# A gated-DeltaNet layer with its out-projection moved behind all heads and two column pairs in seven block products

## The chip, the core and the metric

The kernel runs on one core of one Trainium2 chip. Its time is device microseconds from one launch; the median of three runs counts. Five engines work beside each other and are tied by semaphores: TensorE (PE, matrix products into PSUM), VectorE (DVE), ScalarE (ACT), GpSimd (POOL) and SyncE (SP), whose queue issues every DMA of this kernel in order.

## The reference, cut to what matters

A trunk of two residual layers on x of 1024 tokens by 1024 features, float32, and a final RMSNorm. Layer 0 is a gated DeltaNet (GDN), layer 1 an mLSTM. Each has 8 heads with keys and queries of width 128 and values of width 256.

```python
def gdn_mixer(h, w_in, conv_w, a_log, dt_bias, norm_w, w_out):
    p = h @ w_in                                   # q, k: 1024 columns each; v, z: 2048 each; a, b: 8 each
    ...
    qkv = silu(causal_dwconv(qkv, conv_w))         # 4 taps
    q = l2norm(q) * HEAD_QK ** -0.5;  k = l2norm(k)
    g = -exp(a_log) * softplus(a + dt_bias);  beta = sigmoid(bt)
    o = gated_delta_chunked(q, k, v, g, beta)      # S_t = exp(g)(I - beta k k^T) S_{t-1} + beta k v^T; o = S^T q
    o = rmsnorm(o, norm_w) * silu(z)               # per head
    return o.reshape(B, T, D_INNER) @ w_out        # 2048 x 1024
...
for i in range(DEPTH):
    x = x + mixer_i(rmsnorm(x, norm_w[i]), ...)
return rmsnorm(x, final_norm_w)
```

## The kernel before, in words

Activations lie features first, in tiles of 128 features by 512 tokens: `x[k][half]`, k from 0 to 7, two halves. Every float32 operand of a large product is split into a high part (`hi`, fp32r) and a low part (`lo`, the rest), and a product is three matmuls, hi x hi, hi x lo and lo x hi. `split` (lines 255 to 261) makes the parts of a weight: the high part on ScalarE, the low part on GpSimd. `prenorm` (244) writes the parts `h_hi` and `h_lo` of the normed input.

**One GDN head** projects q, k, two column tiles of v and two of z (`proj_half`, 272: 8 contraction tiles x 3 matmuls for one column tile and half). `conv_silu` (288) reads the sum out of PSUM and does the four taps on VectorE. `gdn_prepare` (536) transposes q and k, forms k k^T and k q^T for eight chunks of 128 tokens and sends the diagonal 32x32 blocks through DRAM (`nt_dram`, then `nd`). `gdn_solve` (606) inverts them with 62 dependent VectorE instructions (lines 615 and 617), sends the result through DRAM (`tb`), and `gdn_merge` (621) joins the blocks to whole 128x128 inverses in four levels of small matmuls (`xp`, `yp`, `xl`, `yl`, line 645). `gdn_scan` (676) then goes over the eight chunks in a chain: `ks` (k times the state S, 702) -> `rr` (VectorE, 704) -> `y` (708) -> `w` (ScalarE, 710) -> `sn` (724) -> the new state `S` (VectorE, 729), with the output `o` (733, 734) beside it. `gate_chunk` (359) transposes a finished chunk, multiplies by the norm weight and silu(z), and splits it into `gg_hi` and `gg_lo`. `out_part` (382) multiplies a half of the head's gated values by the head's 256 rows of the out weights and adds each of eight PSUM tiles into x (VectorE, 399). So the out-projection is done head by head, each a half behind its scan.

**What sets the order.** TensorE's instructions run in the order in which the program emits them (`manual_schedule`); a scheduler orders the other engines. In the GDN layer the order comes from a planner: `gdn_head` is a generator over the next head's units, and between two steps of a scan `pump` takes as many of them as a budget in nanoseconds allows (constants `FA`, `FB`, `FC`; 4500 behind a state), while `out(n)` takes steps of the out-projection. A unit that must wait for a tile names a gate ("mid", "v0", "end", "merge"), which the scan opens. When the next head's units run out, the merge runs with what is left of z between its levels (`ZG`).

**The mLSTM layer** has another form. Its projections are `Pair`s (957): two column tiles, two halves of the tokens and two halves of the contraction make a 2x2 product of blocks, done in seven block products of 12 matmuls (`product`, 949) instead of eight. The sums of input blocks `S1` to `S4` are built once (`h_blocks`, 920, and `last_block`, 938), in the tiles of x, which is kept in DRAM meanwhile; the sums of weight blocks are built per pair. Its out-projection for heads 0 to 6 comes behind all heads (`out_heads`, 1357), from gated values that were stored in DRAM, accumulated over the heads in PSUM. Lists of step numbers (`FIRST`, `UNITS`) say after which block product which piece of scan or preparation comes.

Of the kernel before, what the change touches and what calls it, by code (L numbers as in the profile page):

```python
# [34 lines left out]
PLACES = ((35, 39, 41, 44, 45, 47, 49, 51), (20, 31, 34, 36, 37, 40, 43, 46))  # L35
DECAY = 34
VLO = (((1, 3, 6, 7), (1, 2, 3, 5, 7)), ((3, 6, 7), (1, 3, 5, 7)))
ZM = (24, 17, 15)
ZG = (2, 1, 1)
SECOND = (4, 9)  # L40
P1 = ((), ())
NORM1 = ((-1, 1, 4), (-1, 9, 15))
AHEAD = 6500
MF = 900
RATE0 = 0.5
FS = 1280
OE = 6
ON = (2, 2, 0, 0, 0)
OL = (2, 1, 0, 0, 1)
FA = 600  # L50
FB = 900
FC = 4500
LA = 300
LB = 300
LC = 1280
QB, KB = 4, 3
WB, GB = 2, 2
EP = 0
VT = "ccpp", "ccbb"
B0, B1 = "dc", "d"  # L60
ORDER = "o0 a0 h1 b0 o4 a4 o6 a6 b4 b6"
R8 = range(8)
LOOK = 2
FIRST = {0: "g", 13: "g", 18: "g", 23: "g", 28: "g", 33: "p", 37: "p", 42: "b", 46: "b", 50: "b", 54: "bp", 60: "pr", 68: "s",
# [3 lines left out]
          **{u: "ss" for u in (13, 15, 17, 19, 21, 24, 26)}, 28: "s"})  # L68
# [6 lines left out]
def hybrid_kernel(ctx, tc, x_in, norm_w, final_norm_w, gdn_w_in, gdn_conv_w, gdn_a_log, gdn_dt_bias, gdn_norm_w,  # L75
# [40 lines left out]
    def load_q(w, name):  # L116

        raw = hp.tile([P, KT, P], F32, tag="gate", bufs=GB, name=f"{name}_raw")
        nc.sync.dma_start(raw, w[:, :P].rearrange("(k p) n -> p k n", p=P))
        return raw  # L120
# [95 lines left out]
    def sums_of(accs, name):  # L216

        n = accs[0].shape[1] // P
        cs = pwork(f"{name}_cs", "b")[:, :len(accs) * n]
# [18 lines left out]
    def rows_of(diag, name):  # L238

        rs = pwork(f"{name}_rs", "b")[:, :diag.shape[1] * P]  # L240
        mm(rs, ones, diag.rearrange("p c t -> p (c t)"), start=True, stop=True)
        return rs

    def prenorm(layer, half, diag):
        rs = rows_of(diag, f"n{layer}_{half}")
# [9 lines left out]
    def split(raw, name, tiles=None, e=None):  # L255
# [3 lines left out]
        A.copy(hi, raw)  # L259
        (e or G).tensor_tensor(lo, raw, hi.bitcast(F32), ALU.subtract)  # L260
        return hi, lo
# [3 lines left out]

    def proj(w, c0, name, sink, raw=None):

        parts = split_halves(w, c0, name) if raw is None else raw
        for half in range(2):
            yield from proj_half(parts, name, half, sink)  # L270

    def proj_half(parts, name, half, sink):
        ps = pwork(f"{name}_ps{half}", "p")
        for k in range(KT):
# [5 lines left out]
            yield 640  # L280

    def proj_t(w, c0, n, name):
        res = []
        for _ in proj(w, c0, name, lambda half, ps: res.append(ps)):
            pass
        return res

    def conv_silu(cw, ntile, tl, dst, name):

        col = lambda tap: cw[:, tap * ntile + tl:tap * ntile + tl + 1]  # L290
        last = sp.tile([P, 3], F32, tag="last", bufs=3, name=f"{name}_last")

        def sink(half, ps):
            d_ = dst(half)
            A.activation(d_, ps, AF.Copy, scale=col(3))  # L295
            if half == 0:
                V.tensor_copy(last, ps[:, TH - 3:])
            for d in (1, 2, 3):
                V.scalar_tensor_tensor(d_[:, d:], ps[:, :TH - d], col(3 - d), d_[:, d:], ALU.mult, ALU.add)  # L299
                if half:  # L300
                    V.scalar_tensor_tensor(d_[:, :d], last[:, 3 - d:], col(3 - d), d_[:, :d], ALU.mult, ALU.add)
            A.activation(d_, d_, AF.Silu)
# [3 lines left out]
    def qk_sink(nm, cw, ntile, h, st, name):  # L306
# [6 lines left out]
        return conv_silu(cw, ntile, H + h if nm == "k" else h, dst, f"{name}{nm}{h}")  # L313

    def conv_qk(w, cw, ntile, h, st, name, raws={}):
        for nm, c0 in (("k", QK + h * DK), ("q", h * DK)):
            yield from proj(w, c0, f"{name}{nm}{h}", qk_sink(nm, cw, ntile, h, st, name), raws.get(nm))

    def first_qk(kparts, qraw, gates, cw, ntile, st, name, between, more=()):


        tiles = [wp.tile([P, KT, P], F32R, tag=f"g_{n}", bufs=2, name=f"{name}q0_{n}") for n in ("hi", "lo")]
# [20 lines left out]
    wos = [[] for _ in range(2 * H)]  # L343

    def load_wout(i):

        if i < 2 * H:
            j, h = len(wos[i]), i % H
            w = gdn_w_out[0] if i < H else mlstm_w_out[0]
            pool, tag, bufs = (hp, "acc", 3) if i >= H else (wp, "wraw", WB)  # L350
            raw = pool.tile([P, ET, DV], F32, tag=tag, bufs=bufs, name=f"wo{i}_{j}")
            nc.sync.dma_start(raw, w[h * DV:(h + 1) * DV, j * DV:(j + 1) * DV].rearrange("(e p) n -> p e n", p=P))
            hi = wp.tile([P, ET, DV], F32R, tag="wo_hi", bufs=4, name=f"wo{i}_hi{j}")
            lo = wp.tile([P, ET, DV], F32R, tag="wo_lo", bufs=4, name=f"wo{i}_lo{j}")
            A.copy(hi, raw)  # L355
            G.tensor_tensor(lo, raw, hi.bitcast(F32), ALU.subtract)  # L356
            wos[i].append((hi, lo))

    def gate_chunk(g, gate, parts, cc, nw, name, tag="d"):

        gp = pwork(f"{name}_gp", tag)
# [3 lines left out]
        for e in range(ET):  # L365
            ge, gpe = g[:, e * P:(e + 1) * P], gp[:, e * P:(e + 1) * P]
            if nw is None:
                V.tensor_tensor(ge, gpe, gate[:, e, s_], ALU.mult)
            else:
                V.scalar_tensor_tensor(ge, gpe, nw[:, e:e + 1], gate[:, e, s_], ALU.mult, ALU.mult)  # L370
        g3 = g.rearrange("p (e t) -> p e t", e=ET)
        if parts is None:
            return g3
        hi, lo = parts
        ins = A.copy(hi[:, :, s_], g3)  # L375
        V.tensor_tensor(lo[:, :, s_], g3, hi.bitcast(F32)[:, :, s_], ALU.subtract)  # L376
        return ins

    def gated(name):
        return [wp.tile([P, ET, TH], F32R, tag=f"g_{i}", bufs=2, name=f"{name}_{i}") for i in ("hi", "lo")]  # L380

    def out_part(i, st, c0, n):
# [4 lines left out]
        banks_of = "d" if half == 0 or i % H < H - 1 else B0 if i < H else B1  # L387
        for d in range(KT):
            hi, lo = wos[i][d // 2]
            ds = slice(d % 2 * P, (d % 2 + 1) * P)  # L390
            ps = pwork(f"out{i}_{c0}_{d}", banks_of[d % len(banks_of)])[:, :n * P]
            m = 0
            for e in range(ET):
# [3 lines left out]
                if e < ET - 1:  # L397
                    yield 160 * n
            V.tensor_tensor(x_of(d, c0, n), x_of(d, c0, n), ps, ALU.add)  # L399
            if half and d % 2 and i != H - 1:  # L400
                load_wout(i + 1)
            yield 160 * n
# [26 lines left out]

    hc = lambda t: t.rearrange("p (h c) -> p h c", c=NT)  # L430


    accs = [squares_of(half * HT, HT, f"n0_{half}", "at", 3) for half in range(2)]
# [49 lines left out]
    def gdn_decay():  # L483
# [14 lines left out]
        nc.sync.dma_start(g_dram.rearrange("h (c t) -> (h c) t", t=P), gr_sb)  # L498

    def to_tokens(t, v, e, name):  # L500

        vp = pwork(name)
        for c in range(HT):
            nc.tensor.transpose(vp[:, c * P:(c + 1) * P], t[:, c * P:(c + 1) * P], ident)
        A.copy(v[:, :, e * P:(e + 1) * P], vp.rearrange("p (c d) -> p c d", c=HT))

    def gdn_v(h, st):

        st["vt"], st["v"] = {}, []
        for e in range(ET):  # L510
            def dst(half):
# [3 lines left out]
            yield from proj(gdn_w_in[0], 2 * QK + h * DV + e * P, f"gv{h}_{e}",  # L515
                            conv_silu(gcw, 32, 2 * H + 2 * h + e, dst, f"gv{h}_{e}"))

    def gdn_v_tokens(h, st, half):
        v = hp.tile([P, HT, DV], F32, tag="v", bufs=2, name=f"gv{h}_h{half}")
        st["v"].append(v)  # L520
        for e in range(ET):
            to_tokens(st["vt"][e, half], v, e, f"gvp{h}_{e}_{half}")
        G.tensor_tensor(v, v, st["irk"][:, half * HT:half * HT + HT].unsqueeze(2).to_broadcast([P, HT, DV]), ALU.mult)

    def gdn_z(h, st, e):

        parts = split_halves(gdn_w_in[0], 2 * QK + DI + h * DV + e * P, f"gzp{h}_{e}")

        def sink(half, ps):
            if e == 0:  # L530
                st["gate"].append(hp.tile([P, ET, TH], F32, tag="gate", bufs=GB, name=f"gz{h}_{half}"))
            A.activation(st["gate"][half][:, e, :], ps, AF.Silu)

        return [proj_half(parts, f"gzp{h}_{e}", half, sink) for half in range(2)]

    def gdn_prepare(h, st):

        sk = sp.tile([P, NT], F32, tag="sk", name=f"sk{h}")
        sq = sp.tile([P, NT], F32, tag="sq", name=f"sq{h}")
        b = sp.tile([P, NT], F32, tag="b", name=f"b{h}")  # L540
        irk = sp.tile([P, NT], F32, tag="irk", name=f"irk{h}")
        eq = sp.tile([P, NT], F32, tag="eq", name=f"eq{h}")
        nb = sp.tile([P, NT], F32, tag="nb", name=f"nb{h}")
# [932 lines left out]
```

## Time and profile before

| | |
|---|---|
| median of 3 runs | 2038.01 us (2028.09 to 2044.67) |
| the profiled execution | 2034.36 us, its span 2032.7 us |
| granted TensorE clock, mean over the span | 0.986 |
| instructions | 28574, of them 9912 matmuls |
| moved by DMA | 137.63 MB, mean 68 GB/s |

A profile row names a line of the kernel, an engine, the operation and its tiles (out<-in). A stretch in the tables by windows gives its length, then busy microseconds and (count) of PE, PEld, DVE, ACT and POOL, then the granted clock, the busy share of the 16 DMA engines and GB/s. A row of the waits says which instruction waited for which, the total, how many times, and the longest. A row of the chain gives start, length and what ran.

### The profile page before, as it was taken

The page shows a single profiled execution, that of the slowest core. Times are in us where ns is not written, and L with a number is a line of the kernel's source. Part 1 is how long each engine was busy: PE and PEld are TensorE (multiplying, and loading weights), DVE is VectorE, ACT ScalarE, POOL GpSimd, SP SyncE. Part 2 cuts the span into 40 slices and gives each one's busy share as a digit, 9 for nine tenths or more (in the row PEclk, how much of TensorE's full clock was granted, in tenths as well). Part 3 has the DMA queues.
Part 4 walks back from the last instruction along what each step waited for, and adds up shares of the span by engine and source line. Part 5 has one row for each costly group of instructions (what it writes and reads, how often), then busy time and mean ns, then how long its engine had stood idle before and what let it go on. Part 6 is the DMA issues. An engine that isn't in the chain of part 4 may idle for free.

```text
span 2032.7 us, 28574 instructions
## 1 busy us (share of the span) xinstructions
PE 1934.6 (95%) x9912; PEld 1583.9 (78%) x9912; DVE 1239.5 (61%) x2962; ACT 941.9 (46%) x2108; POOL 682.2 (34%) x621
## 2 busy tenths in 40 slices
PE   5899999999999999999989989999999999999997
PEld 3677787787877878788768768888888888888876
DVE  7666557464584656747576875766666665774313
ACT  5634344343443435334343645455554545464423
POOL 4232232222322223223242234333434343335553
PEclk9999999997999999999989999999999999999999
DMA  4221111121111211111140333522332254346232
GB/s 126 53 71 45 40 54 36 47 55 39 54 34 49 55 40 54 48 45 50 28 130 11 56 79 75 65 70 69 70 76 65 73 57 81 72 160 198 89 116 77
DMA packets 182345, 137.63 MB, mean 68 GB/s; under 512 B 29596, under 2 KB 164280, under 8 KB 182200
## 3 DMA queue, kind: packets, MB, share of 16 engines
q1 hardware_dynamic: 182200, 135.80, 27.4%
q8 instruction: 78, 1.28, 0.3%
q14 instruction: 67, 0.55, 0.1%
HBM read 117.70 MB, written 18.06 MB: 67 GB/s over the span
## 4 chain that ended last, share of the span: by engine, by line
PE 68%; DVE 16%; DMA 6%; ACT 4%; issue 3%; SPq 2%; POOL 1%; DVEq 0%; POOLq 0%; ACTq 0%
PE out L395 7%; PE lout L1375 6%; PE mkq_ps L954 6%; PE mv_ps L954 6%; PE mz_ps L954 6%; PE mog_ps L954 6%; PE gq_ps L277 4%; PE gk_ps L277 4%; PE gv_ps L277 3%; PE gzp_ps L277 3%; DVE xt L617 3%; DVE pr L615 3%; DVE gvT L299 2%; DMA nd<-nt_dram 2%; PE y L708 1%
## 5 line engine op out<-in xcount | busy, mean ns | idle before, releaser
L395 PE MATMUL out<-gg_hi,wo_hi 128*128 128x512 f32 x256 | 124.0, 484 | 2.0 <-ACT gg_hi L375 2.0
L399 DVE TENSOR_TENSOR x<-x,out 128x512 f32<-128x512 f32 x128 | 87.3, 683 | 53.7 <-PE out L395 53.5
L410 POOL TENSOR_TENSOR g_r<-g_r,mhalf 128x1 f32<-128x1 f32 x64 | 35.4, 553 | 242.5 <-DVE g_r L409 240.8
L277 PE MATMUL gv_ps<-hh,gv_hi 128*128 128x512 f32 x256 | 109.7, 428 | 0.5 <-DVE gvT L299 0.3
L277 PE MATMUL gzp_ps<-hh,gzp_hi 128*128 128x512 f32 x256 | 109.0, 426 | 0.0
L395 PE MATMUL out<-gg_lo,wo_hi 128*128 128x512 f32 x256 | 102.5, 401 | 3.1 <-DVE gg_lo L376 3.1
L395 PE MATMUL out<-gg_hi,wo_lo 128*128 128x512 f32 x256 | 102.7, 401 | 0.0
L277 PE MATMUL gzp_ps<-hh,gzp_lo 128*128 128x512 f32 x256 | 101.6, 397 | 0.0
L277 PE MATMUL gzp_ps<-hl,gzp_hi 128*128 128x512 f32 x256 | 101.5, 396 | 0.0
L277 PE MATMUL gv_ps<-hh,gv_lo 128*128 128x512 f32 x256 | 100.6, 393 | 0.0
L277 PE MATMUL gv_ps<-hl,gv_hi 128*128 128x512 f32 x256 | 100.1, 391 | 0.0
L260 POOL TENSOR_TENSOR lw_lo<-lw_raw,lw_hi 128x512 fp32r<-128x512 f32 x56 | 72.7, 1299 | 74.1 <-ACT lw_hi L259 70.2
L260 POOL TENSOR_TENSOR mog_lo<-mog_raw,mog_hi 128x512 fp32r<-128x512 f32 x39 | 50.3, 1290 | 126.6 <-ACT mog_hi L259 78.3
L1375 PE MATMUL lout<-lghh,lw_hi 128*128 128x512 f32 x224 | 89.1, 398 | 0.0
L1375 PE MATMUL lout<-lghl,lw_hi 128*128 128x512 f32 x224 | 87.7, 391 | 0.0
L260 POOL TENSOR_TENSOR mz_lo<-mz_raw,mz_hi 128x512 fp32r<-128x512 f32 x39 | 53.6, 1376 | 98.1 <-ACT mz_hi L259 98.1
L1375 PE MATMUL lout<-lghh,lw_lo 128*128 128x512 f32 x224 | 86.4, 391 | 0.0
L356 POOL TENSOR_TENSOR wo_lo<-wo,wo_hi 128x512 fp32r<-128x512 f32 x36 | 46.2, 1286 | 114.0 <-ACT wo_hi L355 114.0
L615 DVE TENSOR_TENSOR pr<-xt,nd 128x60 f32<-128x60 f32 (+24 forms) x248 | 66.0, 266 | 27.0 <-DMA nd<-nt_dram 21.1
L299 DVE SCALAR_TENSOR_TENSOR gvT<-gv_ps,gcw,gvT 128x511 f32<-128x511 f32 (+2 forms) x96 | 71.2, 741 | 11.5 <-ACT gvT L295 11.3
L260 POOL TENSOR_TENSOR mkq_lo<-mkq_raw,mkq_hi 128x512 fp32r<-128x512 f32 x35 | 46.4, 1326 | 85.7 <-ACT mkq_hi L259 82.2
L375 ACT CAST gg_hi<-gv_h 128x256 fp32r<-128x256 f32 x64 | 25.8, 404 | 103.8 <-DVE gv_h L370 103.6
(599 smaller groups left out, 6246.3 us busy)
## 6 DMA issues: line engine op xcount, KB each, us to landing
lw_raw<-in_mlstm_w_out_dram SPq DMA_DIRECT2D x56, 256.0 KB, 2.8
gv_raw<-in_gdn_w_in_dram SPq DMA_DIRECT2D x32, 256.0 KB, 2.8
gzp_raw<-in_gdn_w_in_dram SPq DMA_DIRECT2D x32, 256.0 KB, 2.8
wo<-in_gdn_w_out_dram SPq DMA_DIRECT2D x32, 256.0 KB, 2.8
mkq_raw<-in_mlstm_w_in_dram SPq DMA_DIRECT2D x28, 256.0 KB, 5.9
mv_raw<-in_mlstm_w_in_dram SPq DMA_DIRECT2D x14, 512.0 KB, 5.2
mg_dram<-mo_g SPq DMA_DIRECT2D x56, 128.0 KB, 3.4
mog_raw<-in_mlstm_w_in_dram SPq DMA_DIRECT2D x14, 512.0 KB, 5.1
```

What stands on the lines that cost most here:

```text
L260: (e or G).tensor_tensor(lo, raw, hi.bitcast(F32), ALU.subtract)
L277: mm(ps, w_[:, k % 4, :], h_[k][half], start=k == 0 and i == 0, stop=k == KT - 1 and i == 2)
L299: V.scalar_tensor_tensor(d_[:, d:], ps[:, :TH - d], col(3 - d), d_[:, d:], ALU.mult, ALU.add)
L356: G.tensor_tensor(lo, raw, hi.bitcast(F32), ALU.subtract)
L375: ins = A.copy(hi[:, :, s_], g3)
L395: mm(ps, a[:, e, ds], b[:, e, hs], start=m == 0, stop=m == 3 * ET - 1)
L399: V.tensor_tensor(x_of(d, c0, n), x_of(d, c0, n), ps, ALU.add)
L410: G.tensor_tensor(r, r, mhalf[:, :1], ALU.pow)
L615: V.tensor_tensor(pr, xt[:, :m, j:j + 1].to_broadcast([P, m, n]), nd[:, j:j + 1, j + 1:].to_broadcast([P, m, n]), ALU.mult)
L617: V.tensor_tensor(xt[:, :m, j + 1:], xt[:, :m, j + 1:], pr, ALU.add)
L954: mm(ps, w_[:, k, :], h_, start=first and k == 0 and i == 0, stop=k == 3 and i == 2, skip_group_check=True)
L1375: mm(pss[2 * j + i], a[:, e, i * P:(i + 1) * P], gs[h * ET + e][b], start=h == 0 and e == 0 and m == 0, stop=h == H - 2 and e == ET - 1 an ...
```

## The change

The GDN layer takes the form of the mLSTM layer, and goes further in the order.

1. The projections become column pairs. Heads 0 and 1 use `Columns` (8 block products, all input blocks as they are). From head 2 on a head has a `Columns` pair of k and the first v tile, and two `Pair`s of seven products: the second v tile with q, and the two z tiles. Because the block of the second half's first features makes room for `S4`, that `Columns` pair works with `S1` and a difference of weights (`sums=True`), still 8 products. `S1`, `S2`, `S3` are built during head 1 (`BLOCKS`), `S4` at its end (`LAST`), in the tiles of x; x is loaded again from the input when the out-projection starts.
2. The out-projection leaves the heads. `gate_chunk` no longer splits; each chunk's gated values go to `gg_dram`. Behind all heads `late` does three runs of `out_heads`: half 0 of heads 0 to 6, half 0 of head 7, half 1 of all heads. `g_parts` loads and splits the gated values; the out weights are loaded once per half, and their `split` multiplies the norm weight in, with two ScalarE and two VectorE instructions a tile (lines 257 to 259 of the new kernel).
3. TensorE's order is a list of steps. Three matmuls make a step: 64 steps for head 0, 96 for head 1, 88 for each later head, 256 for the out-projection. Constants give the step, counted from a head's first, at which keys, queries, solve, merge, tokens and scan emit their next piece. `pump`, `gdn_head` and the gates are gone. Head h's scan runs beside head h+1's products; the last one's beside the out-projection.
4. The order of other engines: `behind()` puts some VectorE and ScalarE instructions behind the scan's latest, and q's convolution is put behind the last instruction of the solve (`st["solved"]`).
5. Smaller: the convolution's three edge columns take fewer instructions; some `Pair` results stay in PSUM (`in_psum`) instead of going to SBUF; weight sums are formed in place; buffers are renamed (`raw`, 3 deep). The mLSTM layer keeps its algorithm and its steps but one; its first norm (`norm1(0)`) now starts at step `second`, where half 1's out-projection begins.

The core of the diff:

```diff
-    def gdn_scan(h, st, outs, pump, opened, last, rate):
+    def gdn_scan(h, st):
...
-                out(steps[0])
-                pump((LA if last else FA) * rate)
+                yield
...
-            hi, lo = parts
-            ins = A.copy(hi[:, :, s_], g3)
+            nc.sync.dma_start(gg_dram[h, :, c * P:(c + 1) * P].rearrange("(e p) t -> p e t", p=P), g3)
...
+        first = Columns(gdn_w_in[0], QK + h * DK, v0, f"gkv{h}", sinks_of(k, vs[0]), sums=h > 1)
+        if h == 1:
+            return [first, Columns(gdn_w_in[0], h * DK, v0 + P, f"gvq{h}", sinks_of(q, vs[1]))]
+        return [first, Pair(gdn_w_in[0], v0 + P, h * DK, f"gvq{h}", sinks_of(vs[1], q))]
...
+        if h < 2:
+            return Columns(gdn_w_in[0], c0, c0 + P, f"gzp{h}", sink, small=h == 0)
+        return Pair(gdn_w_in[0], c0, c0 + P, f"gzp{h}", sink, in_psum=(True, False))
...
+KEYS = ((4, 9, 11, 14), (28, 31, 32, 35), (22, 25, 26, 29))
+QUERIES = ((17, 20, 22, 24), (68, 71, 73, 76), (82, 84, 86, 88))
+SOLVE = (28, 38, 30)
+MERGE = ((78, 82), (88, 94), (86, 100))
+TOKENS = ((37, 39, 81, 85), (71, 74, 97, 103), (64, 68, 107, 110))
+SCAN = (91, 110, 101)
+PACE = ((3, 3, 8), (4, 3, 10), (4, 3, 11))
+BLOCKS = (103, 112, 116, 132)
+LAST = (154, 155, 157, 159)
...
+            b, (l, m, p) = SCAN[i] + base, PACE[i]
+            scan = [b, b + m]
+            for c in range(1, NT):
+                c0 = b + m + p - l - m + p * (c - 1)
+                scan += [c0, c0 + l, c0 + l + m]
+            at_steps(scan + [scan[-1] + 7], gdn_scan(h, st))
...
+        second = end + 16 * H
+        at_steps(range(end - 12, end + 44, 4), parts0)
+        at_steps((end + 64, end + 66), parts1)
+        at_steps([end + 86 + n for n in (*range(0, 16, 2), *range(28, 40, 2), 46, 48)], parts2)
...
+        def late():
+            for half in range(2):
+                load_x(x_src, half)
+            yield from out_heads(0, heads, gs[0], "gout")
+            yield from out_heads(0, (H - 1,), gs[0], "gout7")
+            yield from out_heads(1, range(H), gs[1], "gout")
...
+        for n, _ in enumerate(steps_of(*(c.products() for c in cols), late())):
+            for gen in plan.get(n, ()):
+                do(gen)
+            if n >= second:
+                norm1(0, (n - second) / 4 or -1)
```

In a list of three, the first entry is head 0's, the second head 1's, the third that of all later heads. `PACE` gives, in steps, ks to y, y to sn, and one chunk to the next.

More of the change, by code (lines that the diff above doesn't have):

```diff
@@ new lines, in last_block, with product @@
+    def last_block(temp, e):
+        for k in range(4):
+            a = temp(k)
+            whole(V, a, blocks["A12"][k])
+            add_parts(V, a, a, blocks["S2"][k], ALU.subtract)
+            put("S4", k, a, e)
+            yield
+    def product(ps, block, parts, first=True):
+        hi, lo = parts
+        for k, (bhi, blo) in enumerate(blocks[block]):
+            if k:
+                yield
+            for i, (w_, h_) in enumerate(((hi, bhi), (hi, blo), (lo, bhi))):
+                mm(ps, w_[:, k, :], h_, start=first and k == 0 and i == 0, stop=k == 3 and i == 2,
+                   skip_group_check=True)
@@ new lines, in hybrid_kernel, with ahead, operand, sources_of @@
+    ready, sources = [], []
+    def ahead(n):
+        while len(ready) < n and sources:
+            op = next(sources[0], None)
+            if op is None:
+                sources.pop(0)
+            else:
+                ready.append(op)
+    def operand():
+        ahead(LOOK + 1)
+        return ready.pop(0)
+    def sources_of(pairs):
+        def of(i):
+            if i + 1 < len(pairs):
+                pairs[i + 1].load()
+            yield from pairs[i].operands()
+        return [of(i) for i in range(len(pairs))]
@@ L525, in gdn_z @@
[L525 to L543, printed above, removed]
+            return of
@@ L676, in gdn_scan @@
-    def gdn_scan(h, st, outs, pump, opened, last, rate):
-        S = None
-        st["g"] = []
-        steps = OL if last else ON
-        def out(n):
-            for _ in range(n):
-                if next(outs[0], None) is None:
-                    pump(FS * rate / 2)
+        xp = level("xp", 32, [(32, nt[:32, :, 32:64], t_[:32, :, :32]), (96, nt[64:96, :, 96:], t_[64:96, :, :32])])
+        xs = sp.tile([P, HT, 32], F32, tag="xs", name=f"xs{h}_{half}")
+        A.copy(xs[32:64], xp[32:64])
@@ L821, in hybrid_kernel @@
         mcw, gnw, mnw, fwc = rest[:, :64], rest[:, 64:66], rest[:, 66:68], rest[:, 68:]
[L822 to L841 removed]
+        plan = {}
```

1044 lines of the change are left out of this document (523 added, 521 removed).

## The prediction

> **What bounds the kernel now.** I read the page's engine totals first, then busy time by stretches, then the chain in order of time.
>
> ```profile
> span 2032.7 us, 28574 instructions
> PE 1934.6 (95%) x9912; PEld 1583.9 (78%) x9912; DVE 1239.5 (61%) x2962; ACT 941.9 (46%) x2108; POOL 682.2 (34%) x621
> ```
>
> TensorE is busy 95% of the span, and no other engine is above 61%. That is a mean over stages, and a busy TensorE row counts pipelined matmuls that overlap, so the price of one matmul has to come from start to start. The chain in order of time (start, length, what) gives it, and with it the length of one head in each layer:
>
> ```profile
> 1259.37 2.73 PE mz_ps L954 x12
> 1275.09 5.46 PE mkq_ps L954 x24
> 1366.93 5.46 PE mkq_ps L954 x24
> ...
> 631.24 4.81 PE gk_ps L277 x21
> 753.81 4.81 PE gk_ps L277 x21
> ```
>
> Twelve products of 128x128 by 128x512 take 2.73 us, so one costs 0.2275 us, whatever mean a list of groups shows for it. (gk_ps L277 agrees: 21 in 4.81.) One mLSTM head lasts 1366.93 - 1275.09 = 91.84 us, one GDN head 753.81 - 631.24 = 122.57 us. The same two stretches by engine (length, then busy us and instructions of PE, PEld, DVE, ACT, POOL, then granted clock, DMA share, GB/s):
>
> ```profile
> 631.24:753.81 122.57, 119.09 (x652) 97.09 (x651) 74.46 (x210) 52.04 (x127) 33.28 (x30) 1.00 0.19 48
> 1275.09:1366.93 91.84, 91.45 (x452) 77.01 (x452) 60.31 (x127) 48.76 (x107) 35.34 (x33) 1.00 0.44 69
> 100.00:1050.00 950.00, 913.76 (x4936) 740.86 (x4937) 574.53 (x1607) 395.73 (x967) 260.38 (x236) 0.98 0.19 49
> ```
>
> The mLSTM head, whose projections already are block products in a written order, leaves TensorE idle 0.39 us; the GDN head 3.48 us. So both layers are bound by TensorE, and GDN has a little waiting on top. In a GDN head the reference's four matrices ask for 384 large products (96 for q and k, 96 for v, 96 for z, 96 for the out-projection): 384 x 0.2275 = 87.4 us. The remaining busy time, 119.09 - 87.4 = 31.7 us, is small work: scan, transposes, inverses. Who makes TensorE wait (engine, line, releaser: us in total, times, longest), in the stretch from 250 to 975 us:
>
> ```profile
> PE go_gp L363 <- DVE xt L617: 7.9, 5, 1.6
> PE xp L645 <- DVE t L635: 7.8, 5, 1.6
> PE y L708 <- DVE rr L704: 5.1, 6, 1.9
> ```
>
> All three are one place, the end of `gdn_solve` and the merge, where the next head's products have run out and VectorE has 62 dependent steps to finish: 20.8 us over six heads, 3.5 us a head, the whole idle time.
>
> **The change, part by part.** *Products.* From head 2 on, the pair (v second column, q) and the z pair are `Pair`s: 7 block products of 12 matmuls instead of 8. The third pair, `Columns` with sums, still has 8. That is 6 heads x 2 pairs x 12 = 144 matmuls fewer, and 144 x 0.2275 = **-32.8 us**. Nothing else leaves TensorE: scan, transposes and merges have the same instructions, and the out-projection keeps its 768. Since TensorE is the bound in this stage, this part counts in full. (The Trainium skill, "TensorE: Matmul & The Clock Gate", section "Back-to-back issue gap", gives about 131 ns for a sustained matmul of 512 columns. By it the same 144 would be worth 18.9 us, an estimate; this trace's 227.5 ns disagrees, and the measurement decides.)
>
> *Waits in the steady heads.* The head becomes 88 steps of three products (264 x 0.2275 = 60.1 us) plus 31.7 us of small work, 91.8 us; the 96 out-products move behind all heads. Now every merge level and every scan step has big products before and after it, as in mLSTM. I take 1 us idle per head, between mLSTM's 0.39 and today's 3.48 and nearer the former: 6 x 2.5 = **-15 us**, bounds -19 and 0. The cover for this is the scan's chain. How fast it can go shows in the last head, where ks starts come
>
> ```profile
> 1006.96 0.43 PE ks L702 x2
> 1012.13 0.43 PE ks L702 x2
> ```
>
> 5.2 us apart. The plan gives a chunk 11 steps, 91.8 / 8 = 11.5 us, so a chain step may be over twice as late before TensorE sees it.
>
> *VectorE, ScalarE, GpSimd.* The groups of a GDN head and the mLSTM rows of the same operations (count | busy us, mean ns):
>
> ```profile
> L399 DVE TENSOR_TENSOR x<-x,out 128x512 f32<-128x512 f32 x16 | 10.9, 682 | 7.1 <-PE out L395 7.1
> L617 DVE TENSOR_TENSOR xt<-xt,pr 128x60 f32<-128x60 f32 (+24 forms) x31 | 9.1, 294 | 0.8
> L615 DVE TENSOR_TENSOR pr<-xt,nd 128x60 f32<-128x60 f32 (+24 forms) x31 | 7.6, 244 | 3.2 <-DMA nd<-nt_dram 2.5
> L370 DVE SCALAR_TENSOR_TENSOR gv_h<-go_gp,rest,gz 128x128 f32<-128x128 f32 x16 | 4.9, 344 | 1.4 <-PE go_gp L363 1.4
> L376 DVE TENSOR_TENSOR gg_lo<-gv_h,gg_hi 128x256 fp32r<-128x256 f32 x8 | 4.4, 553 | 1.3 <-ACT gg_hi L375 0.9
> ...
> L983 DVE TENSOR_TENSOR mv_raw<-mv_raw 128x512 f32<-128x512 f32 x1 | 0.7, 694 | 1.2 <-POOL mv_lo L260 1.2
> L1005 DVE TENSOR_TENSOR mkq_u<-mkq_u,mkq_ps 128x512 f32<-128x512 f32 x1 | 0.7, 689 | 1.4 <-PE mkq_ps L954 1.4
> ...
> L259 ACT CAST mv_hi<-mv_raw 128x512 fp32r<-128x512 f32 x6 | 3.7, 622 | 4.4 <-PE mv_ps L954 2.9 <-PE mkq_ps L954 1.4
> ```
>
> Gone from VectorE in a head: 10.9 (x adds, now 24 in all for the layer), 4.4 (gg_lo), about 1.5 (one gating instruction for two). Added by two `Pair`s: 8 operand sums, 4 low parts and 10 sums of products at 0.69 us, 15.2 us, and 1.4 us in `Columns`. So 74.5 - 16.8 + 16.6 = 74 us in 93 us: 80% busy instead of 61%. ScalarE gains 8 splits of 0.62 us and two copies, 52 to at most 59 us. GpSimd keeps 16 low parts a head. All of it fits beside TensorE, so I cost it at nothing; if that cover is gone, it shows as lateness of the solve, the slower rival below.
>
> *Heads 0 and 1.* `h_blocks` and `last_block` put 48 VectorE instructions of 0.69 us, 33 us, into steps 103 to 159. Those 56 steps last about 59 us, and head 1's own VectorE work there is about 59 x 0.6 = 35 us: 68 us for 59. Idle today is 7.4 us here:
>
> ```profile
> 100.00:250.00 150.00, 142.57 (x835) 113.31 (x836) 94.70 (x283) 63.42 (x152) 45.06 (x38) 0.99 0.20 51
> ```
>
> I add **+5 us** (bounds 0, if the scan's slack takes the backlog, and +12).
>
> *The end of the layer.* Today the last head's out-projection, the squares and the norm meet with no products left:
>
> ```profile
> 1020.00:1055.00 35.00, 29.86 (x117) 23.60 (x116) 24.71 (x45) 15.31 (x34) 12.92 (x12) 0.85 0.43 128
> 486.60:507.10 20.50, 20.50 (x127) 14.30 (x127) 2.54 (x7) 4.08 (x10) 2.54 (x2) 0.50 0.12 33
> 1039.50:1049.80 10.30, 9.23 (x26) 7.59 (x27) 3.42 (x5) 2.38 (x4) 5.83 (x6) 0.50 0.39 103
> ```
>
> 5.1 us idle, and 10.3 us at half clock that cost another 5. After the change `norm1(0)` starts at step `second` with 128 steps, 87 us, of products beside it: **-10 us** (bounds -10 and -3). The other stretch at half clock, 20.5 us, lies behind a merge; with products around each merge I count half of its 10 us: **-5 us** (bounds -10 and 0).
>
> *DMA.* The late stage reads x again (16 tiles of 0.25 MB), the gated values (32 such tiles) and each out weight twice, all on SP's queue. The nearest stretch is the mLSTM layer's start of the same routine:
>
> ```profile
> 1810.00:1856.00 46.00, 43.81 (x215) 36.83 (x214) 27.28 (x53) 27.17 (x62) 27.57 (x24) 1.00 0.90 300
> ```
>
> There 300 GB/s ran and TensorE was idle 2.2 us. x alone is 4.2 MB, 14 us at that rate, issued in one go when `late` starts, and the weights behind it are prefetched for three operands, 36 x 0.2275 = 8.2 us. I add **+5 us** (bounds 0 and +10). The out weights' split costs two instructions each on ScalarE and VectorE per 2.73 us of products, about 1 us by the rows above (0.34 us at 128x128, 0.55 us at 128x256): hidden.
>
> *Sum.* -32.8 - 15 + 5 - 10 - 5 + 5 = -53 us. The profiled execution took 2034.4 us (span 2032.7), 3.6 us under the median of 2038.0. So 1981.6 in its terms, and about **1984 us** as a median. All bounds together: -32.8 - 19 - 10 - 10 = -72 (1966) and -32.8 + 12 - 3 + 10 = -14 (2024).
>
> **The rivals.** *Products only (2005 us).* The waits do not vanish but move: VectorE at 80% answers later, and each head keeps its 3.5 us somewhere else. For it: the three waits above are all on VectorE. Against it: the chain needs 5.2 us of 11.5. Time: 2038 - 33 = 2005.
>
> *Full clock and no waits (1954 us).* Every idle us of the stretch 100 to 1050 (950 - 913.8 = 36) goes, and with it the two stretches at half clock, 15 us: 2038 - 33 - 36 - 15. The mechanism is TensorE's activity: the stretches at 0.50 begin where its products thin out. By the Trainium skill ("TensorE: Matmul & The Clock Gate", Part 1: The HAM clock gate) the clock halves only after an idle window of about 3.4 us, which would favour this case, as no such gap would be left. This trace agrees only in part: the 20.5 us began where the longest wait shown above is 1.6 us long.
>
> *SP's queue delays the solve (2077 us, slower).* SP issues in order and now also carries 64 stores of gated values. Its waits today from 250 to 975 us, and the solve's way from `nd` to the first merge product:
>
> ```profile
> SPq L104 <- POOL gzp_lo L260: 124.7, 17, 16.1
> ...
> 573.83 4.42 DMA nd<-nt_dram
> 616.77 0.44 PE xp L645 x15
> ```
>
> From `nd`'s load to xp are 43 us. The plan gives 57 steps (29 to 86), 59 us: 16 us of slack, some 10 once VectorE is at 80%. A weight load that holds SP for 16.1 us ahead of `nt_dram`, with a second wait behind it, makes xp late by 12 us, and `issue_after(solved)` then also holds q's convolution and its PSUM bank. Six heads x 12 = 72 us against 33: 2038 - 33 + 72 = 2077. It turns the change slower from a lateness of 53 / 6 = 9 us a head. Against it: the columns of a pair are asked for one whole pair ahead, 28 to 32 steps.
>
> *The change doesn't do what it says* would show as fewer than 144 matmuls gone; the code leaves no room for it, and I give it no chance of its own.
>
> **How the numbers follow.** A difference under 1%, 20 us, is about what a measurement of this kernel can't tell from none. Forecast (1966 to 1997): 0.55. Products only (1997 to 2015): 0.17. Full clock, no waits (below 1966): 0.13. Losses that eat the gain (2018 to 2058): 0.08. SP's queue, slower: 0.07. Range 1954 to 2015: left out are the last two and some of the third, 0.2. Faster by over 1%: 0.55 + 0.17 + 0.13, less a hundredth at the edge, 0.84; within 1%: 0.09; slower: 0.07.
>
> **What would show it.** The matmul count falls from 9912 to about 9768. The product line of GDN has 12 in 2.73 us. A steady head takes 92 to 94 us, idle under 1.5; over 96 speaks for the first rival, xp waits of many us for the third. The late stage takes 768 x 0.2275 = 175 us and the small work of the last scan. `go_gp` and `xp` no longer lead the waits. No half clock stands at the layer's end. Wrong would make me: a stall at the start of `late` far over 10 us, or VectorE above 90% in a head.

## The result, and the profile after

The changed kernel takes 2051.7 us (median of 8 runs, 2045.9 to 2054.5) against 2037.9 us (8 runs) before: a ratio of 1.0074, 95% interval 1.0049 to 1.0099. It was forecast at 1984. The profiled execution took 2048.3 us. The page after, its span and engine totals:

```profile
span 2046.5 us, 28776 instructions
PE 1919.5 (94%) x9768; PEld 1560.6 (76%) x9768; DVE 1323.2 (65%) x2911; ACT 1039.6 (51%) x2356; POOL 689.1 (34%) x621
```

144 matmuls are gone, as forecast, and yet the span is 14 us longer. Where, is read by stage. The starts of the first products of each stage, in the two timelines, give this account (us):

| stretch | before | after | difference |
|---|---|---|---|
| GDN layer, to the first key product of mLSTM | 1057.4 | 1027.5 | -29.9 |
| mLSTM's first gates and blocks, and heads 0 and 1 | 217.4 | 221.3 | +3.9 |
| **mLSTM heads 2 to 7** (first key product of head 2 to the first product `lout` behind all of `mz`) | 551.7 | 593.7 | **+42.0** |
| last out-projection to the last matmul | 198.0 | 196.3 | -1.7 |

In the kernel before, two single `lout` products run ahead of the last twelve products of `mz`, at 1822.1 us. The expectations below count that stage to the first `lout` of all, which gives 547 us before. The table counts both kernels to the end of the same work.

So the layer that was rewritten gave 30 us, a layer for which the prediction had no term took 42, and the rest is small. Busy time by stretch shows that most of it is waiting (length, then busy us and count of PE, PEld, DVE, ACT, POOL, then clock, DMA share, GB/s). Before, then after:

```profile
1274.80:1826.50 551.70, 549.36 (x2710) 462.54 (x2709) 365.62 (x766) 295.65 (x643) 212.99 (x193) 1.00 0.38 76
```

```profile
1248.80:1842.50 593.70, 564.03 (x2708) 466.65 (x2707) 359.86 (x708) 294.02 (x659) 210.63 (x193) 0.99 0.35 73
```

The same work, but TensorE is idle 29.7 us instead of 2.3. The other 15 us of the 42 lie in its busy time. Part of that is the clock: before, the whole stretch ran at 1.00; after, four stretches at 0.50, 17.0 us together, begin beside waits of 3.1, 3.0, 4.3 and 1.9 us. TensorE is busy for 15.8 us of them, so they cost some 8 us (an estimate: half of that; the chain below has twelve products in 4.37 us at the first of them, 2.72 later). The last 7 us have not been taken apart. Who makes TensorE wait, and whom that engine waits for, in the two answers on waits from 1248 (VectorE: 1250) on, after:

```profile
PE mtp L1343 <- DVE mvlo L1223: 9.6, 8, 3.0
PE mv_ps L471 <- DVE mv_u L587: 6.8, 3, 3.1
PE mz_ps L471 <- DVE mz_u L587: 5.8, 5, 4.3
PE mkq_ps L471 <- DVE mkq_u L587: 4.5, 3, 1.8
```

```profile
DVE mog_raw L557 <- DMA mog_raw<-in_mlstm_w_in_dram: 34.5, 6, 7.8
DVE mv_raw L557 <- DMA mv_raw<-in_mlstm_w_in_dram: 34.4, 6, 7.3
DVE mkq_raw L557 <- DMA mkq_raw<-in_mlstm_w_in_dram: 30.0, 5, 9.4
DVE mz_raw L557 <- DMA mz_raw<-in_mlstm_w_in_dram: 10.9, 5, 4.4
```

TensorE waits for L587, the sum of the running pair's fourth product. VectorE, 61% busy here, isn't short of time: it stands 109.8 us on L557, the first operand sum of the *next* pair, until that pair's weight columns land. Before, no such sum waited for a weight load; one of them waited, once, for a DMA of another kind:

```profile
DVE mog_raw L983 <- DMA mg_dram<-mo_g: 1.2, 1, 1.2
```

The chain after, in one pair, shows the links (start, length, what):

```profile
1285.29 8.37 DMA mog_raw<-in_mlstm_w_in_dram
1293.91 0.45 issue
1294.36 0.69 DVE mv_u L587
1295.10 4.37 PE mv_ps L471 x12
1299.46 0.70 PE mo L1424 x2
1300.74 2.77 PE mv_ps L471 x12
1303.50 2.72 PE mog_ps L471 x12
```

The load for pair `mog` ends, and only then can VectorE do the sum of pair `mv` that TensorE needs. Between them stands L557 for `mog`. The order in which VectorE runs its sums shows it; in the two timelines, around that place (line, result, operands; other instructions left out):

```
before: L1005 mv_u <- mv_u, mv_ps        after: L579 mv_u <- mv_u, mv_ps
        L1013 mv_u <- mv_u, mv_ps               L557 mog_raw <- mog_raw, mog_raw   (needs the whole pair's columns)
        L1019 mv_u <- mv_u, mv_ps               L587 mv_u <- mv_u, mv_ps
        L983  mog_raw <- mog_raw                L593 mv_u <- mv_u, mv_ps
        L984  mog_t <- mog_raw, mog_raw         L558 mog_raw <- mog_raw
        (needs the whole pair's columns)        L599, L607 sums of mv
        L1025, L1032 sums of mv
```

The sum that needs the late columns stands ahead of two of the running pair's product sums before, and of four after.

GDN after, from 100 us on, from the first product of head 2 on, and from that of the out-projection on:

```profile
100.00:239.50 139.50, 125.73 (x714) 101.43 (x713) 114.54 (x285) 71.41 (x162) 51.00 (x39) 0.96 0.18 50
239.50:823.20 583.70, 558.29 (x3123) 446.50 (x3122) 445.88 (x1129) 329.10 (x812) 204.26 (x178) 0.99 0.26 73
823.20:1027.50 204.30, 204.26 (x991) 166.56 (x990) 120.01 (x245) 104.39 (x234) 18.83 (x21) 1.00 0.45 143
```

Heads 2 to 7 last 97 us each, TensorE idle 4.2 us of them (3.5 before); the out-projection runs without a gap at full clock. The waits in the heads are now (PE, 239 to 823 us):

```profile
PE gzp_ps L471 <- ACT gz L809: 8.3, 6, 2.2
PE y L1002 <- DVE xt L925: 3.7, 3, 1.7
PE gzp_ps L471 <- DVE gzp_u L587: 3.5, 3, 1.2
```

### The profile page after: what moved, and what is told of

It reads as the page before. It is cut to its first block, busy times and chain, and to the rows that moved or that the text cites. A ratio compares the mean times of both kernels' runs of the same rounds, so it can differ in the third digit from the quotient of the medians.

```text
span 2046.5 us, 28776 instructions
## 1 busy us (share of the span) xinstructions
PE 1919.5 (94%) x9768; PEld 1560.6 (76%) x9768; DVE 1323.2 (65%) x2911; ACT 1039.6 (51%) x2356; POOL 689.1 (34%) x621
## 4 chain that ended last, share of the span: by engine, by line
PE 41%; DVE 19%; issue 6%; DMA 6%; POOL 4%; ACT 4%; SPq 1%; POOLq 0%; DVEq 0%; ACTq 0%
PE gout L671 9%; PE lout L671 7%; PE mz_ps L471 4%; PE gkv_ps L471 3%; PE mkq_ps L471 3%; PE mog_ps L471 3%; DMA mkq_raw<-in_mlstm_w_in_dram 2%; DVE pr L923 2%; DVE xt L925 2%; PE mv_ps L471 2%; DVE gvT L290 1%; DVE mqT L290 1%; DVE gqT L290 1%; PE mv_ps L1181 1%; DMA mz_raw<-in_mlstm_w_in_dram 1%
## 5 line engine op out<-in xcount | busy, mean ns | idle before, releaser
L259 DVE SCALAR_TENSOR_TENSOR gw_lo<-gw_raw,rest,gw_hi 128x256 fp32r<-128x256 f32 x128 | 60.3, 505 | 58.3 <-ACT gw_hi L258 55.7
L671 PE MATMUL lout<-lgp_hh,lw_hi 128*128 128x512 f32 x224 | 88.5, 395 | 0.4 <-DVE mg L1301 0.3
L258 ACT ACTIVATE gw_hi<-gw_raw,rest 128x256 fp32r<-128x256 f32 x128 | 58.0, 501 | 58.3 <-PE gout L671 36.9
L671 PE MATMUL lout<-lgp_hl,lw_hi 128*128 128x512 f32 x224 | 87.2, 390 | 0.0
L671 PE MATMUL lout<-lgp_hh,lw_lo 128*128 128x512 f32 x224 | 86.3, 390 | 1.0 <-POOL lw_lo L254 1.0
L471 PE MATMUL gkv_ps<-hh,gkv_hi 128*128 128x512 f32 x176 | 78.4, 446 | 0.0
L925 DVE TENSOR_TENSOR xt<-xt,pr 128x60 f32<-128x60 f32 (+24 forms) x248 | 73.8, 298 | 5.5
L254 POOL TENSOR_TENSOR mv_lo<-mv_raw,mv_hi 128x512 fp32r<-128x512 f32 x39 | 52.9, 1357 | 70.5 <-ACT mv_hi L253 45.8
L471 PE MATMUL gkv_ps<-hh,gkv_lo 128*128 128x512 f32 x176 | 70.2, 399 | 0.0
L471 PE MATMUL gkv_ps<-hl,gkv_hi 128*128 128x512 f32 x176 | 70.0, 398 | 0.0
```

The lines of the kernel that those rows point to most:

```text
L258: A.activation(hi[:, k], raw[:, k], AF.Copy, scale=c)
L259: V.scalar_tensor_tensor(lo[:, k], raw[:, k], c, hi.bitcast(F32)[:, k], ALU.mult, ALU.subtract)
L471: mm(ps, w_[:, k, :], h_, start=first and k == 0 and i == 0, stop=k == 3 and i == 2, skip_group_check=True)
L671: mm(pss[2 * j + i], a[:, e, i * P:(i + 1) * P], b, start=h == heads[0] and e == 0 and m == 0, stop=h == heads[-1] and e == ET - 1 and m == 2)
L925: st["solved"] = V.tensor_tensor(xt[:, :m, j + 1:], xt[:, :m, j + 1:], pr, ALU.add)
```

## The experiments

Medians, ratios to the kernel before in the same session, and two lengths from the timelines: mLSTM heads 2 to 7, counted as in the table above, and GDN heads 2 to 7. GDN code that is alike gave 584 to 590 us in five kernels (changed and the four whose names begin with m), so less than some 6 us in that column says nothing. The code cuts are shortened; b_three and b_newform are edits of the kernel before, all others of the changed one.

| kernel | us | ratio, 95% | mLSTM 2-7 | GDN 2-7 |
|---|---|---|---|---|
| changed | 2051.7 | 1.0074 [1.0049, 1.0099] | 593.7 | 583.7 |
| m_buf4 | 2073.7 | 1.0178 [1.0145, 1.0212] | 605.2 | 590.0 |
| m_pin | 2015.6 | 0.9887 [0.9854, 0.9921] | 555.4 | 587.8 |
| m_nopsum | 2063.1 | 1.0128 [1.0086, 1.0169] | 601.3 | 586.2 |
| b_three | 2030.2 | 0.9973 [0.9932, 1.0013] | 551.7 | |
| m_oldform | 2011.2 | 0.9859 [0.9798, 0.9921] | 552.0 | 589.2 |
| b_newform | 2085.7 | 1.0280 [1.0212, 1.0348] | 599.0 | |
| g_pin | 2009.0 | 0.9846 [0.9794, 0.9898] | 556.2 | 582.1 |
| g_nosolve | 1985.5 | 0.9726 [0.9674, 0.9778] | 556.1 | 561.2 |
| g_twice | 2026.7 | 0.9943 [0.9913, 0.9974] | 555.5 | 599.7 |
| x_at | 2019.4 | 0.9909 [0.9876, 0.9942] | 555.1 | 585.6 |
| x_at_gpool | 2029.9 | 0.9978 [0.9955, 1.0002] | 555.1 | 593.0 |
| x_old | 2022.4 | 0.9931 [0.9903, 0.9959] | 551.6 | 594.6 |
| g_spread | 2019.5 | 0.9892 [0.9847, 0.9937] | 555.6 | 593.6 |
| best_old | 2005.6 | 0.9827 [0.9799, 0.9855] | 551.9 | 585.8 |

**Is it the three buffers?** My first theory (A) was that one tag `raw` with 3 buffers, instead of two tags with 2 each, makes the next pair's second half late.

m_buf4:

```
-raw = wp.tile(..., tag="raw", bufs=RAW)             # second half, mLSTM pairs
+b21 = hp.tile(..., tag="kd"); b22 = hp.tile(..., tag="at")  (odd pairs: wp, "raw")
```

> The changed kernel, with the second halves of an mLSTM pair's weight columns (two blocks of 2 KB) in the spare buffers of tags kd, at and raw, so that a whole pair is loaded ahead as before the change; GDN as changed. The stage is from the first key product of mLSTM head 2 to the first product of the last out-projection: 547 us before, 594 us after. Theory A (three buffers under one tag make the next pair's second half late; VectorE, in order, stands on the operand sum L557 that needs it, ahead of the running pair's sums for which TensorE waits): the stage falls to 547-557, the whole to 2007-2016 us. Rival B (the sums left in PSUM hold banks), rival C (the new order of the operand sums) and rival D (the scan step moved from unit 21 to 22): stage 588-596, whole 2046-2056.

b_three:

```
+held = wp.tile(..., tag="g", bufs=4)     # unused, until head 7; pairs' columns: tag "g", bufs=4
```

> The kernel before the change, with the mLSTM pairs' four buffers for weight columns under one tag and one of the four held, unused, from the first pair to the last head: three, as after the change. Nothing else of the change. Theory A: stage (547 before) 570-600, whole 2060-2090 us. Rivals B, C and D: stage 545-551, whole 2034-2042.

Both went against it: with buffers for two whole pairs the changed kernel got *slower* (605 us, above the rivals' figures too), and the kernel before kept its length with three (547 us by the count of the expectation, 551.7 by the table's). In m_buf4 the sum stands ahead of all five product sums of the running pair, one more than as changed. The number of buffers fell as a cause; the place of the sum in VectorE's order took its stead (A2 in what follows).

m_pin:

```
-    V.tensor_tensor(b12, b12, b22, ALU.subtract)
+    with tc.issue_after(added["V"]):      # the newest product sum on VectorE
+        V.tensor_tensor(b12, b12, b22, ALU.subtract)
```

> The changed kernel, with the first operand sum of an mLSTM pair put behind the newest product sum on VectorE; buffers as changed. Theory A: the load is as late as before, but the running pair's sums no longer stand behind it: stage (547 before, 594 after) 552-570, whole 2013-2030 us. If the late load starves TensorE of operands by itself, the stage stays at 580 or more. Rivals B, C and D: stage 588-596, whole 2046-2056.

Measured 555 us: 38 of the 42 us are back, with the loads' buffers as they were. No wait for a weight load is left in VectorE's list, and in that stretch TensorE's whole list of waits for VectorE's sums is

```profile
PE mv_ps L471 <- DVE mv_lo L254: 1.2, 6, 0.2
PE mz_ps L471 <- DVE mz_u L597: 0.5, 1, 0.5
PE mz_ps L471 <- DVE mz_u L591: 0.4, 1, 0.4
```

below 1.9 us for `mtp`, which led with 9.6. The 4 us that remain are back with the old form (below).

m_nopsum (`in_psum=(False, False)` for the key and z pairs):

> The changed kernel, with the mLSTM pairs' second sums written to SBUF as before the change, not left in PSUM. Theory A: stage (547 before, 594 after) 586-598, whole 2045-2058 us. Rival B (banks held): stage 550-570, whole 2010-2030.

601 us: results left in PSUM don't hold TensorE up; with them written to SBUF the stage was 8 us longer, a little above theory A's figure.

**Why did the place change?** The changed pair forms its sums in place: first b12 - b22, which needs nothing but the two loads. The old pair first wrote b12 - b11 over b11, behind the split of b11, and only then needed the second half.

m_oldform:

```
+t2 = hp.tile([P, KT // 2, P], F32, tag="kd", bufs=KB)
+V.tensor_tensor(b11, b12, b11, ALU.subtract)
+V.tensor_tensor(t2, b22, b11, ALU.subtract)
-V.tensor_tensor(b12, b12, b22, ALU.subtract)
-V.tensor_tensor(b11, b11, b12, ALU.subtract)
...
```

> The changed kernel, with the operand sums of the mLSTM pairs in the form they had before the change (first b12 - b11 in place of b11, then b22 minus that into a tile of tag kd); three buffers for the weight columns, sums left in PSUM and all else as changed. In VectorE's order as built, the sum that needs the late second half of the columns then stands ahead of two of the running pair's product sums, as it did before the change; in the changed kernel it stands ahead of four, with the buffers for a whole pair of five, with the pin of one. Theory A2 (that place in VectorE's order is the whole cause, and the place follows from the form): stage 546-556 us (594 as changed), whole 2005-2018. If the late load of three buffers costs by itself: stage 575 or more, whole 2030 or more.

b_newform is the same edit the other way round, in the kernel before:

> The kernel before the change, with the mLSTM pairs' operand sums in the new form (first b12 - b22) and nothing else of the change: four buffers, the GDN layer as before. In VectorE's order as built, this sum then stands ahead of all five product sums of the running pair. Theory A2 with the form alone as the cause: stage 590-610 us (547 before), whole 2080-2100. If the early place hurts only where three buffers also make the load late (form and buffers together): stage 547-555, whole 2036-2048.

Both hit the figures of A2: 552.0 us with the old form in the changed kernel, against 551.7 before the change; and 594.6 by the expectation's count (599.0 by the table's) with the new form in the kernel before, where but for one sign in S3 nothing else was touched and four buffers stood. VectorE's waits there:

```profile
DVE mz_raw L982 <- DMA mz_raw<-in_mlstm_w_in_dram: 20.2, 6, 5.4
DVE mog_raw L982 <- DMA mog_raw<-in_mlstm_w_in_dram: 19.4, 6, 5.3
DVE mkq_raw L982 <- DMA mkq_raw<-in_mlstm_w_in_dram: 19.2, 5, 7.4
```

So the cause of the mLSTM loss is shown from both sides: the form of the operand sums alone. In b_newform TensorE's longest waits go by another way, 23.4 us of `mo` for ScalarE's `mo_g`; which of VectorE's late results stand behind these was not followed. Place and time go together, though not step by step: ahead of one product sum 555 us, at most two 552, four 594 to 601, five 599 to 605. That the new sum moved up *because* the split of b11 no longer stands before it is argued from the code; no run changed that alone.

**Why did GDN give 30 us and not 53?**

g_pin (the pin on GDN's pairs too):

> As m_pin (2015.6 us), with the same pin on the pairs of the GDN layer too, where the sum for the z pair stands ahead of four product sums of the pair before it. If that costs GDN as it cost mLSTM (3 to 7 us a pair): heads 2 to 7 fall from 97 us each to 92-94, whole 1990-2000. If GDN's loads are in time, or its waits come from elsewhere (VectorE's total of work, ScalarE's order): heads 96-98, whole 2010-2018.

582 us against 588: within what alike code scatters. GDN's loads are in time: VectorE's waits for weight columns come to 1.3 us in all of m_pin's heads 2 to 7.

g_nosolve and g_twice start from m_pin and take from VectorE, or give to TensorE.

```
+if 0 < j < BLK - 2: yield; continue                       # g_nosolve, in gdn_solve
+yield from product(p6, "S2", operand(), twice=True)       # g_twice, GDN's pairs
```

> As m_pin, with 58 of the 62 VectorE instructions of the triangular solve left out in every GDN head (16 us a head off VectorE; the output is then another one). Theory V (VectorE, 80 to 85% busy in a head, answers late, and this is the 8 to 9 us that TensorE loses in each of heads 2 to 7): heads fall from 97 us to 89-92, whole 1975-1990. Rival (the scan's and merges' own chain of small products, or half clock, makes the loss): heads 95-97, whole 2005-2015.

> As m_pin, with one block product of 12 matmuls run twice in each of the 12 pairs of GDN: the 144 matmuls that the change took away are back (9912 in all), and no other engine has more to do. Theory T (TensorE's work sets the head, its waits stand beside that): 144 x 0.2275 = 33 us more, whole 2042-2052, heads 102-103 us. Rival (the waits swallow what TensorE is given, as VectorE sets the head): whole 2015-2032, heads 97-100.

Heads 2 to 7 of m_pin, g_nosolve and g_twice:

```profile
234.50:822.30 587.80, 560.25 (x3124) 448.01 (x3123) 448.62 (x1130) 329.05 (x812) 204.57 (x178) 0.99 0.26 73
```

```profile
233.90:795.10 561.20, 551.49 (x3124) 446.03 (x3123) 361.79 (x778) 328.51 (x809) 205.03 (x178) 0.99 0.28 76
```

```profile
239.70:839.40 599.70, 583.55 (x3267) 471.74 (x3266) 437.35 (x1130) 330.43 (x814) 206.26 (x178) 1.00 0.26 72
```

Without the solve a head is 4.4 us shorter, and TensorE's idle time falls from 27.6 to 9.7 us. The time, 1985.5 us, is in theory V's range; a head, 93.5 us, lies between theory and rival. (VectorE is 76% busy in m_pin's heads, not the 80 to 85% of that expectation.) With the 144 matmuls back, 32.8 us of products, the six heads grow by only 11.9, as theory T's rival had it: idle time falls to 16.2 us, busy time grows by only 23.3, and the time at a clock of 0.50 falls from 16.8 to 3.4 us. So in these heads TensorE is no longer the only bound; at the margin its products count for about a third, by a difference that scatters by some 6 us. The whole time agrees: 2026.7 against 2015.6, 11.1 us.

If VectorE's sum of work were the other bound, moving work to GpSimd should help.

```
-V.tensor_tensor(at, grow_b, cmask, ALU.add)     # x_at
+G.tensor_tensor(at, grow_b, cmask, ALU.add)
-Pair(..., engines=(V, V))                       # x_at_gpool and x_old, GDN's pairs
+Pair(..., engines=(G, G))
```

x_old is x_at_gpool with m_oldform's edit besides.

> As g_pin (2009.0 us), with the mask sum of the decay matrix (L863, two a head, 0.9 us each, and 3.3 us a head in which VectorE stands there for the load of growb) moved from VectorE to GpSimd. Theory V (VectorE's lateness sets the GDN heads): heads 2 to 7 fall by 2 to 4 us each, whole 1985-1998. Rival (other work moves up but the solve ends no earlier, or GpSimd's slower sum makes at late): whole 2003-2014.

> As x_at, with the four low parts of operands 6 and 5 of a head's two GDN pairs on GpSimd too (2.8 us a head off VectorE). Theory V: another 1 to 2 us a head, whole 1977-1992. Rival (GpSimd's 1.3 us for a low part makes an operand late for TensorE): equal to x_at or slower, 1990-2015.

> As x_at_gpool, with the old form of the operand sums in the mLSTM pairs in the pin's place (stage 552 us in m_oldform against 555 to 556 with the pin). Theory V and A2: 1973-1990 us, 3 to 4 us under x_at_gpool and under every other kernel here that computes the whole. Rival of x_at_gpool: 1988-2012.

All three missed, the rivals' figures too. From g_pin to x_at to x_at_gpool the rows of heads 2 to 7 read

```profile
238.40:820.50 582.10, 555.53 (x3124) 443.15 (x3123) 445.87 (x1130) 329.51 (x813) 207.55 (x178) 1.00 0.27 74
```

```profile
245.30:830.90 585.60, 557.79 (x3123) 445.51 (x3122) 432.38 (x1117) 345.50 (x824) 216.54 (x188) 0.99 0.26 72
```

```profile
242.50:835.50 593.00, 560.83 (x3123) 449.83 (x3122) 433.83 (x1094) 345.24 (x825) 245.28 (x212) 0.98 0.26 72
```

In x_at VectorE has 13.5 us less to do and the heads aren't shorter (and head 1 took 124.2 us instead of 116.8). In x_at_gpool GpSimd got 28.7 us more, and VectorE did 23 instructions fewer in 1.5 us more: the solve's 372 instructions alone grew from 114.1 to 130.9 us. So x_at_gpool did not lighten VectorE at all, and x_at is the test: VectorE's sum of work is not the bound, and theory V in that form fell.

Last, the place of the solve on VectorE, and the two repairs together.

```
-at_steps(off(SOLVE[i] + n // 2 ...), gdn_solve(h, st))              # g_spread, heads 2 to 7
+at_steps(off(SOLVE[i] + n * 5 // 4 ...), gdn_solve(h, st))
```

> As g_pin (2009.0 us), with the solve's steps of heads 2 to 7 written over 41 steps of TensorE's order instead of 17, so that q's convolution, which is pinned behind the newest solve step, comes ahead of the last third of the solve on VectorE. Theory P (the place of work on VectorE behind the solve makes ScalarE, and through it the z pair's banks, late: 6.8 us of waits on gz and 2.8 on gzp_u in six heads): heads 2 to 7 fall by 1 to 3 us, whole 1990-2003. Rival (the solve's own end, ahead of the merge, is what is late): heads the same or up to 3 us longer, whole 2005-2028.

> The changed kernel with both repairs that worked: the old form of the operand sums in the mLSTM pairs (m_oldform: stage 552 us) and the pin in the GDN pairs (g_pin: heads 2 to 7 1.0 us a head shorter than m_pin). If they add up: 2001-2010 us, under both kernels and under every other run here that computes the whole. If VectorE's order shifts again as it did in x_at (head 1 longer by 7): 2010-2020.

g_spread went the rival's way, 2019.5 us. TensorE's two first waits in GDN's heads, g_spread and then best_old, which has the solve as changed:

```profile
PE xp L956 <- DVE t L947: 8.1, 5, 2.1
PE y L1006 <- DVE xt L929: 5.3, 5, 1.9
```

```profile
PE gzp_ps L471 <- ACT gz L827: 6.8, 6, 1.4
PE gzp_ps L471 <- DVE gzp_u L605: 4.0, 6, 1.2
```

With the solve stretched, the waits on the z pair are gone and those ahead of the merge, which led before the change, are back: the solve is late for one or for the other. best_old, where the two repairs add up, has the lowest median here of those that compute the whole, 2005.6 us, 1.7% under the kernel before; its lead over g_pin, 3.4 us, is within the scatter.

## Why the prediction was wrong

*The step that failed.* Two omissions are one mistake: "All of it fits beside TensorE, so I cost it at nothing", said of VectorE, and no term at all for the mLSTM pairs. The working asks of VectorE only how long its instructions are, not which of them stands in front of which. The diff rewrites the operand sums of the mLSTM pairs, and the list of the change carries it under "smaller". That missing term is +42.0 us, larger than any other in the sum: with the old form of the sums and all else as changed, the kernel takes 2011.2 us (m_oldform) instead of 2051.7. The time fell into "losses that eat the gain", which had a chance of 0.08 and no mechanism. The other half of the mistake cost less and lies in GDN, below.

*Products (-32.8).* The count is exact (9768), and twelve products still take 2.7 us (chain rows of 2.77 and 2.72 us after). Over the whole GDN stretch TensorE's busy time fell by 31.0 us, from 992.7 to 961.7. But "since TensorE is the bound in this stage, this part counts in full" does not hold for the new order: g_twice prices the same 144 matmuls at 11.9 us there.

*Waits in the steady heads (-15).* Nothing of it came: idle 4.2 us a head, forecast 1, today's 3.5. The bounds of -19 and 0 held 0 as an end, and it was passed by some 4 us. The comparison with mLSTM's 0.39 us was wrong, as mLSTM has no solve: with the solve left out, g_nosolve has 1.6 us idle a head. The reading of the old waits was off too: in one head before, `y` waits at 454 us, `go_gp` at 469 and `xp` at 485, so they are three places, and only the last is ahead of the merge.

*VectorE in GDN, costed at nothing.* It is 76% busy in a head, near the 80% forecast, so the sum of work was right and the conclusion wrong. g_nosolve puts the solve at 4.4 us a head, x_at shows that it isn't the sum of VectorE's work, and g_spread shows that moving the solve's steps only moves the wait. What fits all three is the solve's chain of dependent steps, behind and among other sums of 0.7 us; that is argued, and no run changed the chain's length alone. Which of its consumers would have to move to gain these 4.4 us stays open.

*Heads 0 and 1 (+5).* Right, and by the mechanism forecast: idle 13.8 us from 100 to 239.5 against 7.4. One wait makes 6.2 us of it, `yp` for VectorE's `xs` at 144 us, where VectorE is at the sums of input blocks.

*End of the layer (-10), half clock (-5), DMA at the start of `late` (+5).* The first is right: the late stage has 0.04 us idle in 204.3, at a clock of 1.00. The DMA term is nothing: no stall. The clock term came at most in part: 0.99 in heads 2 to 7 after, against 0.98 in the row from 100 to 1050 before, which holds the layer's end too.

*The sum.* GDN made -30 of a forecast -53, near the first rival (33), and its mechanism, "the waits do not vanish but move", fits: TensorE's idle time in GDN was 64.7 us and is 65.8, and the waits of `xp` and `go_gp` gave way to those of the z pair. That the figures agree so closely is partly luck, as the end of the layer gained what heads 0 and 1 and the steady heads lost. (The median forecast is also 1 us low: 2038.0 - 52.8 is 1985.)

*SP's queue (2077).* Its signs, waits of `xp` of many us, aren't there. Yet the idea behind it, one late load that holds an in-order engine ahead of what TensorE needs, is what happened, on VectorE and in the other layer.

## What to carry to other kernels

For each instruction that a change makes ready earlier, ask where it will stand on its engine: a sum whose operands come from a load can be placed ahead of the running work's sums, and everything behind it on that engine then waits for the load as well. Here VectorE stood 110 us on such sums, and the stage grew by 42. Pin such a sum behind the work that the bounding engine waits for; here one such pin was worth 36 us, and more buffers for the load made it worse. Where an engine at 76% has a long dependent chain, read the chain's slack, not the share.

## What the runs showed of the hardware

GpSimd's sums slow VectorE's. In g_pin's timeline (start, length) a step of the solve beside a GpSimd sum, and one before it:

```profile
491.90 0.23 DVE L927 TENSOR_TENSOR pr<-xt,nd 128x70 f32<-128x70 f32 x1
...
494.04 1.31 DVE L927 TENSOR_TENSOR pr<-xt,nd 128x60 f32<-128x60 f32 x1
```

```profile
493.60 1.67 POOL L254 TENSOR_TENSOR gzp_lo<-gzp_raw,gzp_hi 128x512 fp32r<-128x512 f32 x1 [5.82 <-ACT gzp_hi L253]
```

The second ends at 495.35, just after GpSimd's 495.27. Over heads 2 to 7 of that kernel (238.4 to 820.5 us), 274 solve instructions with no GpSimd instruction beside them took 0.21 us on average (at most 0.24), 98 beside one 0.59 (at most 1.77), and the 56 of these beside a GpSimd sum of 128x512 0.87. It fits x_at_gpool, where sums moved to GpSimd left VectorE as busy as it was. The Trainium skill, "SBUF — State Buffer", section "SBUF: two separate sides", says that a VectorE operation with two SBUF inputs and a GpSimd operation that reads SBUF share a port pair under an exclusive lock, and that the loser waits for the whole instruction; these rows agree.
